# RWKV-7 scan: sums in fixed PSUM tiles, inverses spread, the old state added by TensorE and the new one written by ScalarE

## The chip, the cores and the metric

One Trainium2 chip; the kernel runs on one of its cores. The metric is the device time of one execution in microseconds (us). PE is TensorE's matmul, PEld its weight load, DVE VectorE, ACT ScalarE, POOL GpSimd, SP the engine that issues most DMAs. Each engine executes its instructions in the order in which they stand in its queue.

## The reference

Two layers of an encoder, 1024 tokens of width 1024: attention with an MLP, then RWKV-7 time mixing (16 heads of 64, one scan forward and one backward) with an MLP. What the change touches is the recurrence of the scan:

```python
def rwkv7_scan(r, w, k, v, kk, a):
    def step(state, inp):
        r_t, w_t, k_t, v_t, kk_t, a_t = inp
        sa = jnp.einsum('bhvk,bhk->bhv', state, -kk_t)
        state = (state * w_t[:, :, None, :] + sa[..., None] * (kk_t * a_t)[:, :, None, :]
                 + v_t[..., None] * k_t[:, :, None, :])
        return state, jnp.einsum('bhvk,bhk->bhv', state, r_t)
...
    _, out = lax.scan(step, jnp.zeros((nB, H, N, N), F32), xs)
```

## The kernel before

`trunk` runs attention, an MLP, the projections of the RWKV layer (`rwkv_proj`), the scan (`rwkv_scan`), then the output projection and the second MLP. Only `rwkv_scan` is changed.

The scan works in chunks of 64 tokens (`RC`). A batch (`Batch`) is two pairs of heads (`pr`) in two directions (`d`) over half of the sequence; there are 8 (`NB`). A batch has four groups of 128 tokens (`i`), a group two chunks (`c`). So a group holds 8 steps of `scan`, and four chains (`ci = 2 * pr + d`) run beside each other, each with a state `h` of two 64x64 blocks on the diagonal of a 128x128 tile (`hbd`). Chain 0's second chunk needs the state that its first one left, and so on; the chains don't depend on each other.

One step of a chain, L1384 to L1424, with its sums in three column ranges of one PSUM bank `ch` (a tile `c0` to `c3` for each chain):

1. L1384, ACT: `hd` = the old state times the decay `pc`.
2. L1386 and L1390, PE: the chunk's own sum (`af` and `sv`) plus the old state's part (`zr` and `h`).
3. L1392, ACT, and L1393, DVE: the two 64x64 halves of `y` are copied out, one by each engine.
4. L1395, PE: `af` times `y`; L1397, DVE, and L1398, ACT, copy the halves into `sv`.
5. L1401, PE: the state's update from `bn` and `sv`; L1410, DVE (L1407 where there is no old state): for each half `h_new = sum * pc + hd`.
6. L1416 and L1421, PE: the chunk's output, in the same columns as the update; L1424, ACT, copies it to `ot`.

Around the steps runs work that has no place in the chains. `prep` (DVE, POOL, PE, ACT) makes the operands of a group, 8 groups ahead (`NQ` is 9). `invert` makes the inverse of a batch's 64x64 triangles in two halves: a load `nb` (L1290, two DMAs on SP), 30 pairs of DVE operations (L1295, L1297), stores and loads through DRAM that end in `xt` and in `af`. `post` finishes the inverse on PE (L1350, L1361) before the group's first step. `finish` normalises and stores.

What sets the order: the code is traced step by step. After each step, `side()` lets `b1` (prep), `b2` (post, and what is left of the inverse) and `b3` (finish) go one piece on; at a group's end all three are drained. The whole DVE part of the next batch's inverse is traced at the second group of a batch (L1513 to L1517). A scheduler then orders the traced instructions of each engine by a model of time, with the steps of the scan ahead of the rest (`tc.high_priority(50)`). It also keeps the accesses of different engines to one PSUM bank in the order of the trace.

Of the kernel before, what the change touches and what calls it, by code (L numbers as in the profile page):

```python
# [25 lines left out]
def fsl(i, n):  # L26
    return slice(i * n, (i + 1) * n)
# [1115 lines left out]
def rwkv_scan(tc, g, ap, dr, yd):  # L1143
# [7 lines left out]
    with ExitStack() as es:  # L1151
# [35 lines left out]


        hbd = [[t1.tile([P, P], F32, name=f"h{d}{i}") for i in range(2)] for d in range(4)]
        ybd = [t1.tile([P, 2, RC], F32, name=f"y{d}") for d in range(4)]  # L1190
        for x in sum(hbd, ybd):
            nc.gpsimd.memset(x, 0.0)
        bk = t1.tile([P, 4, 2, 2, RC], F32, name="bk")
        for j in range(2):
            nc.gpsimd.memset(bk[fsl(1 - j, 64), :, j], 0.0)
# [90 lines left out]
        def invert(q):  # L1286

            nb = ip.tile([P, 32, 32], F32, tag="nb", name="nb")
            for i in range(2):
                nc.sync.dma_start(out=nb[fsl(i, 64)], in_=q.nd.rearrange("j u s t -> (j u) s t")[:, fsl(i, 32), fsl(i, 32)])  # L1290
            tmp = ip.tile([P, 512], F32, tag="xtmp", name="xtmp")
            for t in range(30, 0, -1):
                n = 31 - t
                tv = tmp[:, :t * n].rearrange("p (a b) -> p a b", b=n)
                nc.vector.tensor_tensor(out=tv, in0=nb[:, 0:t, t:t + 1].to_broadcast([P, t, n]),  # L1295
                                        in1=nb[:, t:t + 1, t + 1:32].to_broadcast([P, t, n]), op=ALU.mult)
                li = nc.vector.tensor_tensor(out=nb[:, 0:t, t + 1:32], in0=nb[:, 0:t, t + 1:32], in1=tv, op=ALU.add)  # L1297
                if t % 2 == 0:
                    yield
# [67 lines left out]
        def scan(q, i, hs, side):  # L1367
# [3 lines left out]
            for c in range(2):  # L1371
                for pr in range(2):
                    for d in range(2):
                        with tc.high_priority(50):
                            ci = 2 * pr + d
                            u = 2 * pr + c
                            zr, bn, af, pc, sv = w.zr[d][:, u], w.bn[d][:, u], w.af[:, d, u], w.pc[d], w.sv[:, d, u]
                            h = hs[ci]
                            ch = psC.tile([P, 512], F32, tag=f"c{ci}", name=f"c{ci}")
                            last = q.half == 1 and i == 3 and c == 1  # L1380
                            y = ybd[ci]
                            if h is not None and not last:
                                hd = hp.tile([P, P], F32, tag=f"hd{ci}", name=f"hd{ci}", bufs=1)
                                nc.scalar.activation(hd, h, AF.Copy, scale=pc[:, u:u + 1])  # L1384
                            for j in range(2):
                                nc.tensor.matmul(ch[fsl(1 - j, 64), 0:64], lhsT=af[:, j, 0:64], rhs=sv[:, j, :],  # L1386
                                                 start=True, stop=h is None)
                            if h is not None:
                                for j in range(2):
                                    nc.tensor.matmul(ch[fsl(1 - j, 64), 0:64], lhsT=zr[:, 0, :], rhs=h[:, fsl(j, 64)],  # L1390
                                                     start=False, stop=True)
                            nc.scalar.activation(y[0:64, 1], ch[0:64, 0:64], AF.Copy)  # L1392
                            nc.vector.tensor_copy(y[64:128, 0], ch[64:128, 0:64])  # L1393
                            for j in range(2):
                                nc.tensor.matmul(ch[fsl(1 - j, 64), 64:128], lhsT=af[:, j, 0:64], rhs=y[:, j], start=True,  # L1395
                                                 stop=True)
                            nc.vector.tensor_copy(sv[64:128, 0, :], ch[64:128, 64:128])  # L1397
                            nc.scalar.activation(sv[0:64, 1, :], ch[0:64, 64:128], AF.Copy)  # L1398
                            if not last:
                                for j in range(2):  # L1400
                                    nc.tensor.matmul(ch[fsl(j, 64), 128:192], lhsT=bn[:, j, :], rhs=sv[:, j, :], start=True,  # L1401
                                                     stop=True)
                                hn = hbd[ci][c]
                                for j in range(2):
                                    rows = cols = fsl(j, 64)
                                    if h is None:
                                        nc.vector.tensor_scalar(out=hn[rows, cols], in0=ch[rows, 128:192],  # L1407
                                                                scalar1=pc[rows, u:u + 1], scalar2=None, op0=ALU.mult)
                                    else:
                                        nc.vector.scalar_tensor_tensor(out=hn[rows, cols], in0=ch[rows, 128:192],  # L1410
                                                                       scalar=pc[rows, u:u + 1], in1=hd[rows, cols],
                                                                       op0=ALU.mult, op1=ALU.add)
                                hs[ci] = hn

                            for j in range(2):
                                nc.tensor.matmul(ch[fsl(j, 64), 128:192], lhsT=sv[:, j, :], rhs=af[:, j, 64:128],  # L1416
                                                 start=True, stop=h is None)
                            if h is not None:
                                for j in range(2):
                                    rows = fsl(j, 64)  # L1420
                                    nc.tensor.matmul(ch[rows, 128:192], lhsT=h[:, rows], rhs=zr[:, 1, :], start=False,  # L1421
                                                     stop=True)
                            o = w.ot[:, 0, pr, c, :] if d == 0 else w.ot[:, 1, pr, 1 - c, ::-1]
                            nc.scalar.activation(o, ch[:, 128:192], AF.Copy)  # L1424
                        side()
# [79 lines left out]
        for G in range(4 * NB):  # L1505
# [4 lines left out]
            g2 = G + NQ - 1  # L1510
            if G == 0:
                q.gi = gi
            if i == 1 and b + 1 < NB:  # L1513
                bn = bs[b + 1]
                bn.gi = invert(bn)
                while not hasattr(bn, "inv"):
                    next(bn.gi)  # L1517
            if g2 < 4 * NB:
                if g2 % 4 == 0:
                    bs.append(Batch(g2 // 4))  # L1520
# [1 line left out]
            if G + 1 < 4 * NB:  # L1522
                if i == 0:
                    b2.add(post(q, 1), q.gi)
                else:
                    b2.add(post(bs[(G + 1) // 4], (G + 1) % 4))
            if i == 1 and b + 1 < NB:
                b2.add(first(bn))
            n = [0]

            def side():
                n[0] += 1
                b1.step()
                b2.step()
                b3.step()
                if n[0] == 8:
                    b1.drain()
                    b2.drain()
                    b3.drain()
# [159 lines left out]
```

## Time and profile before

| | |
|---|---|
| median of 3 runs | 3665.36 us (3656.43 to 3675.8) |
| profiled execution | 3664.62 us, span from first to last instruction 3662.9 us |
| busy in the span | PE 87%, PEld 71%, DVE 69%, ACT 50%, POOL 48% |
| first and last output copy of the scan (L1424) | 2086.4 and 2859.9 us |
| mean granted PE clock | 0.912 of full speed |

A row of a group reads: line, engine, operation, tile written <- tiles read, shape, count | busy us, mean ns of one | idle us of the engine just ahead of them, with what ended it. Instructions of one engine overlap, so busy time can be less than count times mean. A 64x64 f32 matmul has two records.

### The profile page before, as it was taken

What the parts mean: (1) busy time and instruction counts of PE and PEld (TensorE: products, weight loads), DVE (VectorE), ACT (ScalarE), POOL (GpSimd) and SP (SyncE); (2) the same over time, 40 slices, a digit from 0 to 9 for tenths busy, and PEclk for the clock granted to TensorE, in tenths of its full rate; (3) what the DMA queues carried; (4) which work ended last, traced back from release to release, by engine and by line L of the source; (5) the groups of instructions that cost most, each with busy time, mean ns of one, the idle gap of its engine ahead of it and who ended that gap; (6) DMA issues with size and microseconds to landing.
All of it is one profiled execution on the core that took longest, in us unless ns stands there. A gap on an engine that the chain in (4) does not pass through costs nothing. (4 is left out here: it accounts for less than half of the span.)

```text
span 3662.9 us, 61199 instructions
## 1 busy us (share of the span) xinstructions
PE 3175.4 (87%) x22168; PEld 2587.1 (71%) x22168; DVE 2529.6 (69%) x4649; ACT 1849.7 (50%) x4244; POOL 1768.2 (48%) x1610
## 2 busy tenths in 40 slices
PE   7999998899999888888887687788777889999988
PEld 6788887688777676665566566666665768877766
DVE  3355564744499978977855778887776474449996
ACT  2366564455543347754433365555666445554333
POOL 1000001465598884455566344444431156558887
PEclk9999998899999998999896687778887899999999
DMA  6222214232231133257765354445444423323113
GB/s 202 72 80 81 72 55 171 76 138 108 70 139 37 79 113 107 95 185 232 228 221 155 94 127 107 106 127 122 121 100 133 129 84 135 115 71 131 42 74 115
DMA packets 408204, 425.70 MB, mean 116 GB/s; under 512 B 138155, under 2 KB 321579, under 8 KB 401756
## 3 DMA queue, kind: packets, MB, share of 16 engines
q1 hardware_dynamic: 406716, 417.58, 36.3%
q0 software_dynamic: 1184, 4.20, 0.4%
q8 instruction: 174, 2.85, 0.3%
q14 instruction: 130, 1.06, 0.1%
HBM read 290.83 MB, written 138.20 MB: 117 GB/s over the span
## 5 line engine op out<-in xcount | busy, mean ns | idle before, releaser
L101 PE MATMUL pm<-bhi,lo 128*128 128x512 f32 x840 | 331.8, 398 | 49.5 <-DVE lo L130 49.3
L130 DVE TENSOR_TENSOR lo<-x,hi 128x512 fp32r<-128x512 f32 x300 | 323.3, 1084 | 62.4 <-ACT hi L129 62.0
L129 ACT ACTIVATE hi<-x 128x512 fp32r<-128x512 f32 x300 | 189.1, 631 | 334.1 <-PE pm L100 129.1
L100 PE MATMUL pm<-blo,hi 128*128 128x512 f32 x840 | 330.2, 393 | 7.7 <-POOL blo L130 7.3
L99 PE MATMUL pm<-bhi,hi 128*128 128x512 f32 x840 | 319.2, 393 | 7.1 <-ACT bhi L129 6.7
L127 POOL TENSOR_TENSOR x<-w1r 128x512 f32<-128x512 f32 x160 | 214.6, 1345 | 203.1 <-DVE lo L130 178.3
L130 POOL TENSOR_TENSOR blo<-bx,bhi 128x512 fp32r<-128x512 f32 x138 | 221.1, 1603 | 30.5 <-ACT bhi L129 29.7
L1268 POOL TENSOR_TENSOR af<-af,amask 128x512 f32<-128x512 f32 x128 | 164.8, 1293 | 147.2 <-ACT af L1267 109.3
L101 PEld LDWEIGHTS pm<-bhi,lo 128*128 128x128 f32 x840 | 157.6, 188 | 101.9 <-DVE lo L130 70.8
L1264 PE MATMUL A<-zr,bk 128*128 128x128 f32 x1024 | 189.5, 349 | 44.3 <-DVE bk L1257 38.2
L905 POOL TENSOR_TENSOR wl<-wr,wh 128x512 fp32r<-128x512 f32 (+2 forms) x144 | 162.0, 1136 | 126.3 <-ACT wh L904 94.8
L127 POOL TENSOR_TENSOR bx<-w 128x512 f32<-128x512 f32 x140 | 215.1, 1539 | 9.5
L1264 PEld LDWEIGHTS A<-zr,bk 128*128 128x128 f32 x1024 | 168.1, 252 | 57.2 <-POOL bk L1258 22.0
L127 DVE TENSOR_TENSOR x<-h 128x512 f32<-128x512 f32 x140 | 195.6, 1409 | 5.3 <-ACT h L268 2.7
L100 PEld LDWEIGHTS pm<-blo,hi 128*128 128x128 f32 x840 | 158.4, 189 | 47.7 <-POOL blo L130 14.5
L99 PEld LDWEIGHTS pm<-bhi,hi 128*128 128x128 f32 x840 | 158.4, 189 | 40.0 <-ACT bhi L129 7.6
L99 PE MATMUL mm<-xmh,wh 128*128 128x512 f32 x384 | 163.0, 443 | 10.1 <-ACT wh L904 4.7
L1416 PE MATMUL c<-af,sv 128*64 128x64 f32 x1024 | 96.8, 273 | 74.7 <-DVE h L1410 67.7
L1410 DVE SCALAR_TENSOR_TENSOR h<-c,pc,hd 64x64 f32<-64x64 f32 x448 | 127.0, 284 | 49.6 <-PE c L1401 28.7
L583 ACT ACTIVATE S<-S,mneg 128x256 f32<-128x256 f32 (+2 forms) x256 | 124.7, 499 | 69.1 <-DVE mneg L578 46.2
L335 DVE TENSOR_TENSOR acc<-acc,pm 128x512 f32<-128x512 f32 x256 | 158.1, 675 | 0.3 <-PE pm L101 0.3
L886 DVE SCALAR_TENSOR_TENSOR x<-u,mu,x 128x512 f32<-128x512 f32 x192 | 153.4, 832 | 7.0 <-ACT x L884 4.3
(369 smaller groups left out, 9933.0 us busy)
## 6 DMA issues: line engine op xcount, KB each, us to landing
w1r<-in_mlp_w_dram SPq DMA_DIRECT2D x32, 1024.0 KB, 5.5
w<-in_mlp_w_dram SPq DMA_DIRECT2D x32, 1024.0 KB, 6.7
x<-x SPq DMA_DIRECT2D x64, 386.0 KB, 3.3
hd<-h SPq DMA_DIRECT2D x24, 1024.0 KB, 4.2
h<-hd SPq DMA_DIRECT2D x24, 1024.0 KB, 8.2
wr<-in_w_rkv_dram SPq DMA_DIRECT2D x96, 256.0 KB, 2.8
x<-xo SPq DMA_DIRECT2D x32, 512.0 KB, 3.7
rk<-rk SPq DMA_DIRECT2D x64, 256.0 KB, 3.7
```

The costliest lines, as they stand in the source:

```text
L99: nc.tensor.matmul(out, lhsT=ahi, rhs=bhi, start=start, stop=False)
L100: nc.tensor.matmul(out, lhsT=ahi, rhs=blo, start=False, stop=False)
L101: nc.tensor.matmul(out, lhsT=alo, rhs=bhi, start=False, stop=stop)
L127: add.tensor_tensor(out=y, in0=x, in1=blocks[term[2]], op=ALU.add if term[1] == "+" else ALU.subtract)
L129: nc.scalar.activation(hi, x, AF.Copy)
L130: sub.tensor_tensor(out=lo, in0=x, in1=hi, op=ALU.subtract)
L335: dve.tensor_tensor(out=a, in0=a, in1=banks[j], op=ALU.add if sign == "+" else ALU.subtract)
L886: nc.vector.scalar_tensor_tensor(out=x, in0=at(2 * i), scalar=mu[:, i, c, kt:kt + 1], in1=x, op0=ALU.mult, op1=ALU.add)
L905: nc.gpsimd.tensor_tensor(out=wlo, in0=wr, in1=whi, op=ALU.subtract)
L1264: nc.tensor.matmul(ps[:, fsl(u, P)], lhsT=bk[:, u, j].rearrange("p a b -> p (a b)"), rhs=zr[:, u].rearrange("p a b -> p (a b)"), start=Tru ...
L1268: nc.gpsimd.tensor_tensor(out=o, in0=o, in1=consts["amask"].unsqueeze(1).to_broadcast([P, 4, P]), op=ALU.mult)
L1410: nc.vector.scalar_tensor_tensor(out=hn[rows, cols], in0=ch[rows, 128:192], scalar=pc[rows, u:u + 1], in1=hd[rows, cols], op0=ALU.mult, op ...
```

## The change

The four banks `chs` are taken once and set to 0 by DVE. `y` is one 128x128 tile for the two halves, the first sums go to a block each of a 128x128 range whose other two blocks stay 0, and ACT copies it in one instruction. The old state is added on PE, by a matmul with the identity into the columns of the update (256 to 384), and ACT multiplies the sum by `pc` and writes the new 128x128 state; `hd` and DVE's part in the state are gone. `af y` goes to columns 192 to 256. The output keeps columns 128 to 192, now apart from the update. The DVE part of the next batch's inverse is traced in pieces: its load after the batch's first step, two of the 30 pairs after each of the steps 4 to 18, the rest with the DMAs after step 20.

```diff
--- before.py
+++ after.py
@@ -1187,9 +1187,13 @@
 
 
         hbd = [[t1.tile([P, P], F32, name=f"h{d}{i}") for i in range(2)] for d in range(4)]
-        ybd = [t1.tile([P, 2, RC], F32, name=f"y{d}") for d in range(4)]
-        for x in sum(hbd, ybd):
+        yst = [t1.tile([P, 2, RC], F32, name=f"y{d}") for d in range(4)]
+        for x in sum(hbd, []):
             nc.gpsimd.memset(x, 0.0)
+
+        chs = [psC.tile([P, 512], F32, name=f"c{d}") for d in range(4)]
+        for x in chs:
+            nc.vector.memset(x, 0.0)
         bk = t1.tile([P, 4, 2, 2, RC], F32, name="bk")
         for j in range(2):
             nc.gpsimd.memset(bk[fsl(1 - j, 64), :, j], 0.0)
@@ -1289,6 +1293,7 @@
             for i in range(2):
                 nc.sync.dma_start(out=nb[fsl(i, 64)], in_=q.nd.rearrange("j u s t -> (j u) s t")[:, fsl(i, 32), fsl(i, 32)])
             tmp = ip.tile([P, 512], F32, tag="xtmp", name="xtmp")
+            yield
             for t in range(30, 0, -1):
                 n = 31 - t
                 tv = tmp[:, :t * n].rearrange("p (a b) -> p a b", b=n)
@@ -1376,42 +1381,31 @@
                             u = 2 * pr + c
                             zr, bn, af, pc, sv = w.zr[d][:, u], w.bn[d][:, u], w.af[:, d, u], w.pc[d], w.sv[:, d, u]
                             h = hs[ci]
-                            ch = psC.tile([P, 512], F32, tag=f"c{ci}", name=f"c{ci}")
+                            ch = chs[ci]
                             last = q.half == 1 and i == 3 and c == 1
-                            y = ybd[ci]
-                            if h is not None and not last:
-                                hd = hp.tile([P, P], F32, tag=f"hd{ci}", name=f"hd{ci}", bufs=1)
-                                nc.scalar.activation(hd, h, AF.Copy, scale=pc[:, u:u + 1])
+                            y = yst[ci]
+                            rs = [fsl(1 - j, 64) for j in range(2)]
                             for j in range(2):
-                                nc.tensor.matmul(ch[fsl(1 - j, 64), 0:64], lhsT=af[:, j, 0:64], rhs=sv[:, j, :],
+                                nc.tensor.matmul(ch[rs[j], fsl(j, 64)], lhsT=af[:, j, 0:64], rhs=sv[:, j, :],
                                                  start=True, stop=h is None)
                             if h is not None:
                                 for j in range(2):
-                                    nc.tensor.matmul(ch[fsl(1 - j, 64), 0:64], lhsT=zr[:, 0, :], rhs=h[:, fsl(j, 64)],
+                                    nc.tensor.matmul(ch[rs[j], fsl(j, 64)], lhsT=zr[:, 0, :], rhs=h[:, fsl(j, 64)],
                                                      start=False, stop=True)
-                            nc.scalar.activation(y[0:64, 1], ch[0:64, 0:64], AF.Copy)
-                            nc.vector.tensor_copy(y[64:128, 0], ch[64:128, 0:64])
+                            nc.scalar.activation(y.rearrange("p j t -> p (j t)"), ch[:, 0:P], AF.Copy)
                             for j in range(2):
-                                nc.tensor.matmul(ch[fsl(1 - j, 64), 64:128], lhsT=af[:, j, 0:64], rhs=y[:, j], start=True,
-                                                 stop=True)
-                            nc.vector.tensor_copy(sv[64:128, 0, :], ch[64:128, 64:128])
-                            nc.scalar.activation(sv[0:64, 1, :], ch[0:64, 64:128], AF.Copy)
+                                nc.tensor.matmul(ch[rs[j], 192:256], lhsT=af[:, j, 0:64], rhs=y[:, j], start=True, stop=True)
+                            nc.vector.tensor_copy(sv[64:128, 0, :], ch[64:128, 192:256])
+                            nc.scalar.activation(sv[0:64, 1, :], ch[0:64, 192:256], AF.Copy)
                             if not last:
+                                if h is not None:
+                                    nc.tensor.matmul(ch[:, 256:384], lhsT=g.ident, rhs=h, start=True, stop=False)
                                 for j in range(2):
-                                    nc.tensor.matmul(ch[fsl(j, 64), 128:192], lhsT=bn[:, j, :], rhs=sv[:, j, :], start=True,
-                                                     stop=True)
+                                    nc.tensor.matmul(ch[fsl(j, 64), 256 + 64 * j:320 + 64 * j], lhsT=bn[:, j, :], rhs=sv[:, j, :],
+                                                     start=h is None, stop=True)
                                 hn = hbd[ci][c]
-                                for j in range(2):
-                                    rows = cols = fsl(j, 64)
-                                    if h is None:
-                                        nc.vector.tensor_scalar(out=hn[rows, cols], in0=ch[rows, 128:192],
-                                                                scalar1=pc[rows, u:u + 1], scalar2=None, op0=ALU.mult)
-                                    else:
-                                        nc.vector.scalar_tensor_tensor(out=hn[rows, cols], in0=ch[rows, 128:192],
-                                                                       scalar=pc[rows, u:u + 1], in1=hd[rows, cols],
-                                                                       op0=ALU.mult, op1=ALU.add)
+                                nc.scalar.activation(hn, ch[:, 256:384], AF.Copy, scale=pc[:, u:u + 1])
                                 hs[ci] = hn
-
                             for j in range(2):
                                 nc.tensor.matmul(ch[fsl(j, 64), 128:192], lhsT=sv[:, j, :], rhs=af[:, j, 64:128],
                                                  start=True, stop=h is None)
@@ -1510,11 +1504,9 @@
             g2 = G + NQ - 1
             if G == 0:
                 q.gi = gi
-            if i == 1 and b + 1 < NB:
+            if i == 0 and b + 1 < NB:
                 bn = bs[b + 1]
                 bn.gi = invert(bn)
-                while not hasattr(bn, "inv"):
-                    next(bn.gi)
             if g2 < 4 * NB:
                 if g2 % 4 == 0:
                     bs.append(Batch(g2 // 4))
@@ -1524,8 +1516,6 @@
                     b2.add(post(q, 1), q.gi)
                 else:
                     b2.add(post(bs[(G + 1) // 4], (G + 1) % 4))
-            if i == 1 and b + 1 < NB:
-                b2.add(first(bn))
             n = [0]
 
             def side():
@@ -1533,6 +1523,13 @@
                 b1.step()
                 b2.step()
                 b3.step()
+
+                at = 8 * i + n[0]
+                if b + 1 < NB and (at == 1 or 4 <= at <= 18):
+                    next(bn.gi)
+                if at == 20 and b + 1 < NB:
+                    for _ in first(bn):
+                        pass
                 if n[0] == 8:
                     b1.drain()
                     b2.drain()
```

The built order of PE in the middle of the scan, before. `c_` with a number is the bank of one step; `y_17480` to `y_17483` and `h_17472` to `h_17479` belong to chains 0 to 3.

```order
L1401 MATMUL c_23117<-sv,bn_19857 64x64 x2
L1401 MATMUL c_23237<-sv,bn_20302 64x64 x2
L1386 MATMUL c_23318<-sv,af 64x64 x2
L1390 MATMUL c_23318<-h_17475,zr_20301 64x64 x2
L1416 MATMUL c_23088<-af,sv 64x64 x2
L1421 MATMUL c_23088<-zr_19854,h_17476 64x64 x2
L1416 MATMUL c_23117<-af,sv 64x64 x2
L1421 MATMUL c_23117<-zr_19855,h_17478 64x64 x2
```

PE at about the same place in the changed kernel, where `c_17492` to `c_17495` are the four fixed banks.

```order
L1410 MATMUL c_17494<-af,sv 64x64 x2
L1415 MATMUL c_17494<-zr_20083,h_17477 64x64 x2
L1355 MATMUL B<-xt,af 32x32 x5
L1280 MATMUL A<-ident,bk 128x64 x3
L1410 MATMUL c_17495<-af,sv 64x64 x2
L1415 MATMUL c_17495<-zr_20084,h_17479 64x64 x2
L1402 MATMUL c_17492<-h_17472,ident 128x128
L1404 MATMUL c_17492<-sv,bn_20085 64x64 x2
L1397 MATMUL c_17493<-y_17481,af 64x64 x2
```

The identity matmul (L1402) stands just ahead of the update's (L1404); the output's (L1410, L1415) still come after the update of their own step.

DVE before, where an inverse (L1295, L1297) meets the steps:

```order
L1397 COPY sv<-c_19970 64x64
L1410 SCALAR_TENSOR_TENSOR h_17474<-c_19912,pc_18017,hd_19913 64x64 x2
L1297 TENSOR_TENSOR nb<-nb,xtmp 128x30
L1257 TENSOR_TENSOR bk<-x,ipr 64x4x64
L1295 TENSOR_TENSOR xtmp<-nb 128x58
L1257 TENSOR_TENSOR bk<-x,ipr 64x4x64
L1297 TENSOR_TENSOR nb<-nb,xtmp 128x29x2
L1295 TENSOR_TENSOR xtmp<-nb 128x84
L1297 TENSOR_TENSOR nb<-nb,xtmp 128x28x3
L1295 TENSOR_TENSOR xtmp<-nb 128x108
L1410 SCALAR_TENSOR_TENSOR h_17476<-c_19970,pc_18016,hd_19971 64x64 x2
```

DVE after, at such a place again:

```order
L1398 COPY sv<-c_17492 64x64
L1300 TENSOR_TENSOR xtmp<-nb 128x220
L1398 COPY sv<-c_17493 64x64
L1302 TENSOR_TENSOR nb<-nb,xtmp 128x20x11
L1261 TENSOR_TENSOR bk<-x,ipr 64x4x64
L1300 TENSOR_TENSOR xtmp<-nb 128x228
L1398 COPY sv<-c_17494 64x64
L1261 TENSOR_TENSOR bk<-x,ipr 64x4x64
L1302 TENSOR_TENSOR nb<-nb,xtmp 128x19x12
L1300 TENSOR_TENSOR xtmp<-nb 128x234
L1302 TENSOR_TENSOR nb<-nb,xtmp 128x18x13
```

The steps leave DVE one copy each (L1398); the halves of `y` and of the state are gone from its queue.

ACT before:

```order
L1398 ACTIVATE sv<-c_22694 64x64
L1267 ACTIVATE af<-A 128x4x128
L1424 ACTIVATE ot<-c_22658 128x64
L1392 ACTIVATE y_17482<-c_22723 64x64
L1278 ACTIVATE bn_22463<-A 128x4x64
L1392 ACTIVATE y_17483<-c_22752 64x64
L1278 ACTIVATE bn_22463<-A 128x4x64
L1384 ACTIVATE hd_22873<-h_17475,pc_19859 128x128
L1392 ACTIVATE y_17480<-c_22791 64x64
L1339 ACTIVATE sv<-B 64x8x64 x2
```

ACT after, in the same part of the scan:

```order
L1407 ACTIVATE h_17479<-c_17495,pc_19413 128x128
L1399 ACTIVATE sv<-c_17492 64x64
L1399 ACTIVATE sv<-c_17493 64x64
L1395 ACTIVATE y_17482<-c_17494 128x128
L1271 ACTIVATE af<-A 128x4x128
L1418 ACTIVATE ot<-c_17495 128x64
L1407 ACTIVATE h_17472<-c_17492,pc_19734 128x128
L1435 ACTIVATE osq<-ot 128x512
L1407 ACTIVATE h_17474<-c_17493,pc_19735 128x128
L1399 ACTIVATE sv<-c_17494 64x64
```

L1384 (`hd`) is gone; L1407, the new state, now stands in the queue between the copies of other chains, and L1395 copies all of `y`.

## The prediction

> **What bounds the kernel now.** The change touches only the scan stage, so I first placed that stage in the span, with the view of one source line (the copy of a step's output, L1424, one per chain and step; columns: count, duration ns min/median/max, first and last start) and with the busy time of the engines in that stretch (length, then PE, PEld, DVE, ACT, POOL busy, PE clock, DMA share, GB/s).
>
> ```profile
> L1424 ACT ACTIVATE ot<-c x256: 197/220/235, 2086.4 to 2859.9; 128x64 f32<-128x64 f32 x128
> 2088.00:2862.00 774.00, 614.63 (x9966) 499.19 (x9967) 598.77 (x1708) 463.26 (x1553) 287.49 (x356) 0.80 0.45 116
> ```
>
> The stage is 774 us of the 3662.9. PE is busy 79% of it, DVE 77%, ACT 60%: no engine is full, so waits count. Busy time in shorter stretches shows two regimes. First five that hold the bulk of an inverse, then two with almost none of it; under the sum of the five stands the same sum for L1397 alone, which runs once per step.
>
> ```profile
> 2205.00:2269.50 64.50, 48.47 (x644) 40.02 (x643) 54.14 (x142) 35.39 (x118) 23.29 (x29) 0.72 0.38 104
> 2615.00:2674.00 59.00, 43.74 (x694) 35.54 (x692) 51.69 (x144) 33.89 (x113) 24.54 (x31) 0.83 0.44 111
> sum 293.50, PE 226.94 PEld 186.20 DVE 257.18 ACT 165.88 POOL 119.93; mean PE 45.39 PEld 37.24 DVE 51.44 ACT 33.18 POOL 23.99
> sum 293.50, DVE 17.99; mean DVE 3.60
> 2490.00:2509.00 19.00, 17.02 (x358) 14.41 (x357) 12.81 (x39) 12.99 (x48) 10.71 (x14) 1.00 0.63 153
> 2694.00:2709.00 15.00, 15.00 (x277) 12.76 (x276) 9.14 (x30) 10.28 (x35) 9.34 (x10) 0.97 0.55 122
> ```
>
> In the five (293.5 us) DVE is busy 257.2, 88%, against PE's 77%: DVE sets the pace. In the two short ones PE is busy 90% and 100%, DVE 67% and 61%. The waits of the stage (engine and line that waited, for whom: us, times, longest) say the same:
>
> ```profile
> ACT hd L1384 <- DVE h L1410: 96.9, 115, 4.1
> ACT sv L1398 <- DVE sv L1397: 77.7, 91, 3.7
> PE c L1416 <- DVE h L1410: 67.7, 78, 4.4
> PE c L1395 <- DVE y L1393: 37.3, 41, 5.0
> PE c L1401 <- ACT sv L1398: 25.3, 31, 2.8
> ```
>
> PE's three largest waits, 130.3 us of its 159 idle, end with a chain's DVE copy (the last through ACT, which waits for DVE's half of `sv`). That DVE was busy elsewhere, not slow, shows in the timeline of one such wait (start, duration): chain 0's ACT half of `y` (ACT L1392) is done at 2355.97, its DVE half starts at 2360.20.
>
> ```profile
> 2355.77 0.20 ACT L1392 ACTIVATE y<-c 64x64 f32<-64x64 f32 x1
> ```
> ```profile
> 2357.48 0.94 DVE L1252 TENSOR_TENSOR zr<-x,rk 128x256 f32<-128x256 f32 x1
> 2358.34 0.32 DVE L1295 TENSOR_TENSOR xtmp<-nb 128x168 f32<-128x168 f32 x1
> 2358.59 0.86 DVE L1257 TENSOR_TENSOR bk<-x,ipr 64x256 f32<-64x256 f32 x2
> 2359.48 0.33 DVE L1297 TENSOR_TENSOR nb<-nb,xtmp 128x168 f32<-128x168 f32 x1
> 2359.85 0.32 DVE L1295 TENSOR_TENSOR xtmp<-nb 128x150 f32<-128x150 f32 x1
> 2360.20 0.23 DVE L1393 COPY y<-c 64x64 f32<-64x64 f32 x1
> ```
>
> **The change part by part.** Durations come from groups of the stage (busy us, mean ns | idle before it):
>
> ```profile
> L1410 DVE SCALAR_TENSOR_TENSOR h<-c,pc,hd 64x64 f32<-64x64 f32 x448 | 127.0, 284 | 49.6 <-PE c L1401 28.7 <-ACT y L1392 4.2 <-PE c L1390 2.6
> L1393 DVE COPY y<-c 64x64 f32<-64x64 f32 x252 | 54.1, 226 | 21.5 <-ACT y L1392 18.2
> L1407 DVE TENSOR_SCALAR h<-c,pc 64x64 f32<-64x64 f32 x24 | 6.8, 283 | 1.9 <-PE c L1401 0.9 <-PE c L1416 0.6
> L1384 ACT ACTIVATE hd<-h,pc 128x128 f32<-128x128 f32 x220 | 87.5, 399 | 107.7 <-DVE h L1410 96.9 <-DVE h L1407 8.4
> L1424 ACT ACTIVATE ot<-c 128x64 f32<-128x64 f32 x255 | 53.6, 216 | 16.0 <-PE c L1421 12.7 <-PE c L1416 0.3 <-PE c L1386 0.2
> L1392 ACT ACTIVATE y<-c 64x64 f32<-64x64 f32 x252 | 51.2, 211 | 24.4 <-PE c L1390 22.1
> L1278 ACT ACTIVATE bn<-A 128x256 f32<-128x256 f32 x92 | 33.6, 373 | 5.1 <-PE A L1276 4.8
> L1267 ACT ACTIVATE af<-A 128x512 f32<-128x512 f32 x92 | 52.8, 590 | 28.4 <-PE A L1264 19.5 <-PE c L1416 8.2 <-issue 0.2
> L1445 ACT ACTIVATE osq<-L,gneps 128x512 f32<-128x512 f32 x31 | 21.2, 683 | 20.8 <-PE L L1443 20.6
> L1264 PE MATMUL A<-zr,bk 128*128 128x128 f32 x736 | 125.0, 325 | 4.7 <-DVE zr L1252 1.8 <-DVE bk L1257 1.4 <-DVE xtmp L1295 0.5
> ```
>
> DVE loses 127.0 + 54.1 + 6.8 = 188 us of work, 598.8 to 411 (53% of 774). A step loses 2 x 284 + 226 = 794 ns of DVE and one whole hand-over (`y` went ACT, then DVE).
>
> ACT loses `hd` (87.5) and gains the new state, 128x128 from PSUM with a scale per partition. That form isn't in the trace. 128x64 takes 216 and 128x256 takes 373, so 128x128 lies on the line between them at 268; a per-partition operand adds 683 - 590 = 93 (L1445 against L1267): 361 ns, bounds 268 and 399 (`hd`, the same shape with the same kind of scale). 248 of them are 89.5 us. `y` as one 128x128 copy costs 268 - 211 = 57 more, 252 times, 14 us. ACT goes 463 to 480: no change of load, but it now stands in the chain four times a step.
>
> PE gains 224 identity matmuls 128x128 in f32. The nearest is L1264, also 128x128 f32: its 736 records are two for each matmul, 125.0 / 736 = 0.17 us each, so 0.34 us a matmul and 76 us in all (615 to 691, 89%). In the new order it stands directly ahead of the state's own matmuls and behind the same wait for `sv`, so it can't run early, and lies on the chain.
>
> What does not change: the sums of one chain still share one bank, in the built order the output matmul still waits for the copy of the state (now ACT's), and the next step's first matmul for the output copy. Fixed tiles alone remove no wait; I cost them at 0. The spread inverses keep all 60 DVE operations of a batch. The load of `nb`, two DMAs that hold SP's queue (below), moves up by up to a group, past loads for groups far ahead; its DVE work ends 1 to 7 steps earlier in the order. The wait that could shorten is that of the post-inverse matmuls for `xt`:
>
> ```profile
> 2401.44 5.18 SPq L1290 DMA_DIRECT2D nb<-nd  x2
> L1350 PE MATMUL B<-xt,af 32*32 32x32 f32 x960 | 29.6, 203 | 3.5 <-ACT sv L1339 2.3 <-DMA xt<-xd 1.1
> 1947.73 1.04 DVE L1250 TENSOR_TENSOR zr<-x,rk 128x256 f32<-128x256 f32 x1 [2.87 <-DMA y<-y]
> ```
>
> 1.1 us in all: -1 at best; if the earlier `nb` load held the loads behind it for its whole 5.18 us in each of 7 batches, +36. I take 0, nearest the row, as those loads have whole groups to spare. The four memsets of the banks (DVE, 128x512, once) stand before the third `prep`, where DVE idles 2.87 us (last row): 0, at most 3.
>
> **The sum.** (1) In the five DVE-bound stretches, 17.99 us / 226 ns = 80 steps lose 80 x 794 = 64 us of DVE. PE has 293.5 - 226.9 = 67 us of idle there for 80 x 0.34 = 27 of identity work. I take three quarters, -48 (bounds 0 and -64), since other waits then end last. (2) In the other 480 us the share of the 130.3 us of DVE-made PE waits is 480/774, 81 us; the copy comes from a less loaded queue, or from ACT, and I take half, -40 (bounds 0 and -81). (3) The other 144 identities cost 49 us of PE; PE's remaining idle takes half: +24 (bounds 0 and +49). (4) The longer `y`: 63 steps of a chain x 57 ns, +4. Together -60: 3664.6 (the profiled execution's time; the median of the runs, 3665.4, is the same) - 60 = **3605 us**.
>
> Two rules of the Trainium skill bear on the size. Its page Perfetto Trace Analysis, Identifying the Most-Contended Engine, says that matmul busy time is a bad measure of PE's headroom; by that the 89% would overstate PE, term (3) would be near 0 and the time 3581. The trace agrees as far as the two short stretches go (PE 90% and 100% "busy" at 19 and 15 us for about the same work).
>
> **The rivals.** *PE takes over.* If PE's busy time is real occupancy, terms (1) and (2) are eaten by the 76 us: -48 - 40 + 76 + 4 = -8, 3657, no change. For it: PE is at 90 to 100% in the short stretches. Against it: the same kind of work took 15 us in one and 19 in the other with PE nominally full in both.
>
> *The clock rises too.* PE's clock is 0.72 in a stretch with long waits and 1.00 in one without; at 0.80 on average it stretches every matmul. If the shorter waits lift it to 0.90, PE's 615 us become 546, 68 less, of which half lies on the path: another -34, 3571; all of it, 3537. I take 3550. For it: waits of 4 to 5 us (4.4 and 5.0 in the rows) are just the ones that go. Against it: 2205 to 2269 and 2615 to 2674 have the same DVE share and clocks of 0.72 and 0.83. The Trainium skill, TensorE: Matmul & The Clock Gate, Part 1, has the mechanism: half clock by default and after an idle window of about 3.4 us, full clock after a busy one.
>
> *ACT's queue becomes the bound: slower.* ACT runs in order and stops at its half of `sv` until DVE's half is done: 77.7 us over 91 stops, 0.85 each. Now the new state stands in that queue, behind other chains' `sv`. If each of a chain's 62 states meets one such stop, that is 62 x 0.85 = 53 us, and the identity is 56 x 0.34 = 19; the loop is shorter by 226 + 568 - 361 - 57 = 376 ns, 62 times, -23. Net +49: 3714. It decides once the state waits longer at ACT than it did at DVE by 376 - 340 = about 40 ns beyond what the lighter DVE queue gives back. Against it: DVE, for which ACT stops, loses a third of its work, and the largest stop, `hd`'s 96.9 us, goes.
>
> **How the numbers follow.** Forecast (about 3575 to 3640) 0.50; clock 0.20; PE takes over 0.17; ACT 0.13. Below 0.5% (18 us) a measurement can't tell the two apart. Faster: the first two and a little of the third, 0.74; same 0.14; slower 0.12. The range reaches from the sum with the far ends of (1) and (2), 3664.6 - 64 - 81 = 3520, a little lowered for the clock, 3515, to 3662, which takes in most of "PE takes over" and leaves the slower rival out.
>
> **What would show it.** In the changed kernel's profile: the stage from the first to the last output copy some 60 us shorter; DVE 410 us there; the identity at 0.17 us a record; the state's copy at about 360 ns; no long waits of PE for DVE. The inverse stretches should shrink most and the PE-full ones hardly. I am wrong if the stretches with the inverse keep 55 to 60 us, if ACT's new waits are as long as DVE's were, or if PE's clock moves by more than 0.05.

## The result, and the profile after

The changed kernel takes 3605.73 us (median of 4 runs, 3597.65 to 3608.16), 0.9833 of the time before, with an interval of 0.9802 to 0.9864: about 61 us less. Its profiled execution took 3597.65 us, with a span of 3595.9 us and a PE clock of 0.933 over the span (before 3664.62, 3662.9 and 0.912). A profile is of one execution, here the fastest of the four, and for e3 and e11 below the slowest of four, so small differences between two profiles say little.

First the stage again, in the changed kernel, with the two views that placed it before: the copy of a step's output, and busy time by stretch (length, then PE, PEld, DVE, ACT, POOL, PE clock, DMA share, GB/s). The second and third stretch split the stage: the first seven batches, beside each of which the next batch's inverse runs, and the last batch, which has none beside it.

```profile
L1418 ACT ACTIVATE ot<-c x256: 197/224/269, 2085.2 to 2792.0; 128x64 f32<-128x64 f32 x128
```
```profile
2085.00:2792.00 707.00, 648.65 (x10416) 528.08 (x10414) 420.18 (x960) 466.91 (x1567) 289.66 (x355) 0.90 0.49 127
2085.00:2733.00 648.00, 597.12 (x9446) 487.70 (x9446) 397.25 (x907) 422.60 (x1417) 280.60 (x347) 0.90 0.50 125
2733.00:2792.00 59.00, 51.54 (x974) 40.38 (x972) 22.94 (x53) 44.31 (x151) 9.06 (x9) 0.97 0.47 143
```

The same two stretches of before:

```profile
2086.00:2800.00 714.00, 567.38 (x9076) 463.16 (x9078) 560.85 (x1589) 422.65 (x1414) 281.32 (x348) 0.80 0.46 115
2800.00:2860.00 60.00, 47.23 (x908) 35.79 (x906) 39.73 (x126) 41.35 (x143) 5.59 (x7) 0.83 0.38 120
```

The stage is 67 us shorter, all of the 67 us between the two profiled executions. The seven batches with an inverse beside them give 66 of these (714 to 648 us), the last one 1 (60 to 59). DVE falls from 77% busy to 59%, PE rises from 79% to 92% and ACT from 60% to 66%. The clock rises from 0.80 to 0.90.

Second the groups that the change made or touched (us busy, mean ns | idle before, by whom ended), and under them the stage's waits (engine and line that waited, for whom: us, times, longest):

```profile
L1402 PE MATMUL c<-h,ident 128*128 128x128 f32 x448 | 117.5, 347 | 31.1 <-ACT sv L1399 30.6
L1268 PE MATMUL A<-zr,bk 128*128 128x128 f32 x736 | 116.9, 306 | 3.7 <-DVE zr L1256 2.5 <-DVE bk L1261 0.9
L1407 ACT ACTIVATE h<-c,pc 128x128 f32<-128x128 f32 x236 | 84.7, 364 | 57.9 <-PE c L1404 56.4
L1410 PE MATMUL c<-af,sv 128*64 128x64 f32 x1008 | 82.8, 244 | 4.7 <-ACT sv L1399 2.6 <-ACT h L1407 1.7
L1389 PE MATMUL c<-sv,af 128*64 128x64 f32 x1000 | 82.4, 243 | 7.2 <-ACT ot L1418 7.2
L1395 ACT ACTIVATE y<-c 128x128 f32<-128x128 f32 x252 | 65.3, 270 | 12.4 <-PE c L1393 8.3 <-PE c L1389 1.8 <-PE c L1404 0.5
```
```profile
DVE sv L1398 <- PE c L1397: 94.1, 64, 5.4
ACT sv L1399 <- DVE sv L1398: 89.4, 67, 4.9
ACT h L1407 <- PE c L1404: 56.4, 96, 2.8
PE c L1402 <- ACT sv L1399: 30.6, 22, 3.7
```

The direction of the waits has turned. Before, PE's longest waits ended with a DVE copy (67.7, 37.3 and 25.3 us); now DVE waits 94 us and ACT 56 us for PE, and PE has one wait of size left, the 30.6 us ahead of the identity. Both new ACT copies take what was worked out for them, 364 ns (361) and 270 ns (268). The identity does not: 117.5 us busy over 448 records is 0.26 us each, where the prediction had 0.17 from L1264.

### The profile page after: what moved, and what is told of

It reads as the page before. It is cut to its first block, busy times and chain, and to the rows that moved or that the text cites. A ratio compares the mean times of both kernels' runs of the same rounds, so it can differ in the third digit from the quotient of the medians.

```text
span 3595.9 us, 61432 instructions
## 1 busy us (share of the span) xinstructions
PE 3213.8 (89%) x22616; PEld 2618.0 (73%) x22616; DVE 2357.0 (66%) x3917; ACT 1853.7 (52%) x4260; POOL 1778.8 (49%) x1606
## 5 line engine op out<-in xcount | busy, mean ns | idle before, releaser
L1268 PE MATMUL A<-zr,bk 128*128 128x128 f32 x1024 | 181.1, 336 | 44.5 <-DVE bk L1261 40.1
L1268 PEld LDWEIGHTS A<-zr,bk 128*128 128x128 f32 x1024 | 158.5, 238 | 54.8 <-POOL af L1272 21.5
L1261 DVE TENSOR_TENSOR bk<-x,ipr 64x256 f32<-64x256 f32 x128 | 118.2, 924 | 70.8 <-PE A L1280 62.2
L1398 DVE COPY sv<-c 64x64 f32<-64x64 f32 x256 | 55.2, 226 | 163.9 <-PE c L1397 94.1
```

The lines of the kernel that those rows point to most:

```text
L1268: nc.tensor.matmul(ps[:, fsl(u, P)], lhsT=bk[:, u, j].rearrange("p a b -> p (a b)"), rhs=zr[:, u].rearrange("p a b -> p (a b)"), start=Tru ...
```

## The experiments

Each ran beside the kernel before on the same chip, and each ratio, with its 95% interval, is against that; a gain in us is the ratio's share of 3665. "Stage" is from the first to the last output copy, read as above.

### The identity, taken out and put in

**e1: the changed kernel without the identity.** What is left out of the new state is the old one.

```diff
-if h is not None:
-    nc.tensor.matmul(ch[:, 256:384], lhsT=g.ident, rhs=h, start=True, stop=False)
 for j in range(2):
     nc.tensor.matmul(ch[fsl(j, 64), 256 + 64 * j:320 + 64 * j], lhsT=bn[:, j, :], rhs=sv[:, j, :],
-                     start=h is None, stop=True)
+                     start=True, stop=True)
```

> The changed kernel without the identity matmul: the old state is left out of the new one, all else is computed. In the changed kernel's profile the identity is busy on PE for 117.5 us of a stage of 707, and PE is busy 92% of it. Theory PE is full: it is paid nearly in full, at least 80 us go, about 3505 to 3525. Theory of the prediction (half of it lies in PE's idle time): 40 to 60 us go, 3545 to 3565. Theory clock (PE's clock rose from 0.80 to 0.90 because PE is denser): with less work it falls back to 0.80 to 0.85, and only 15 to 35 us go, 3570 to 3590.

Measured: 3564.83 us, 0.9732 [0.9714, 0.9750]. Its stage:

```profile
2084.00:2751.00 667.00, 553.32 (x9966) 460.05 (x9966) 403.87 (x959) 455.02 (x1567) 290.74 (x356) 0.88 0.53 136
```

In its place the identity costs 0.0101 of the time, 37 us (41 by the two medians), a third of its 117.5 us of busy time. All else together brought 98 us.

**e7: the kernel before, with the identity added** into columns that nothing reads.

```diff
 if not last:
+    if h is not None:
+        nc.tensor.matmul(ch[:, 256:384], lhsT=g.ident, rhs=h, start=True, stop=True)
```

> The kernel before with the same identity matmul added into columns of the bank that nobody reads; nothing else changes, DVE keeps its work. It is on the chain as in the change. Theory PE is full everywhere: 76 to 117 us more, 3740 to 3780. Theory of the prediction (DVE sets the pace, PE has 159 us of idle): 25 to 45 more, 3690 to 3710. Theory clock: the denser PE gets a clock of 0.85 or more in the stage and that pays it back, 3650 to 3675.

Measured: 3696.40 us, 1.0088 [1.0073, 1.0103], 32 us more. The stage, and the identity in it:

```profile
2088.00:2890.00 802.00, 710.56 (x10426) 568.33 (x10426) 588.17 (x1715) 465.85 (x1555) 288.24 (x355) 0.84 0.44 112
```
```profile
L1401 PE MATMUL c<-h,ident 128*128 128x128 f32 x448 | 128.0, 374 | 11.0 <-ACT sv L1398 10.4
```

In the kernel before PE had 159 us of idle in the stage, and yet 128 us of busy time cost 32: idle time of PE on the average does not cover an instruction that stands in each chain. The clock rose by 0.04 and didn't pay for it.

**e2: the changed kernel, the identity in two blocks of 64x64** (the state's other two blocks are 0).

```diff
-    nc.tensor.matmul(ch[:, 256:384], lhsT=g.ident, rhs=h, start=True, stop=False)
+    for j in range(2):
+        nc.tensor.matmul(ch[fsl(j, 64), 256 + 64 * j:320 + 64 * j], lhsT=g.ident[fsl(j, 64), fsl(j, 64)],
+                         rhs=h[fsl(j, 64), fsl(j, 64)], start=True, stop=False)
```

> The changed kernel with the identity matmul only on the two 64x64 blocks that hold the state, one matmul for each, which as other such pairs should run beside each other: about half of PE's time for it, 60 us less. Theory PE is full: 45 to 60 us go, 3545 to 3560. Theory of the prediction: 20 to 30, 3575 to 3585. Theory clock: under 15, 3590 to 3605.

Measured: 3606.86 us, 0.9846 [0.9829, 0.9862], no gain. The stage, and the identity in it:

```profile
2092.00:2802.00 710.00, 635.71 (x10862) 520.05 (x10858) 426.59 (x960) 465.86 (x1567) 287.78 (x355) 0.87 0.49 126
```
```profile
L1403 PE MATMUL c<-h,ident 64*64 64x64 f32 x896 | 80.3, 256 | 16.2 <-ACT sv L1399 16.1
```

The identity's busy time falls by 37 us, but PE's by 13 only, and the clock from 0.90 to 0.87: the rest of PE's work took 24 us more. (Over the whole span the changed kernel's four runs have clocks of 0.927 to 0.933 and those of e2 0.924 to 0.926, so the clock is lower in e2, but by less.) If PE's busy time set the end, a third of 37 us or more would have come back. Why it did not stays open; the lower clock goes with it, but the run cannot say which of the two is the cause.

### One part of the change at a time

**e8: the kernel before, with the four fixed banks alone.**

```diff
+chs = [psC.tile([P, 512], F32, name=f"c{d}") for d in range(4)]
+for x in chs:
+    nc.vector.memset(x, 0.0)
...
-ch = psC.tile([P, 512], F32, tag=f"c{ci}", name=f"c{ci}")
+ch = chs[ci]
```

> The kernel before with nothing but the four fixed banks (and their memsets). Prediction: the order of the accesses to a bank is the same, so no change, 3655 to 3675. Rival: the release of a whole tile held the next step's first matmuls, 3630 or less.

Measured: 3666.59 us, 1.0001 [0.9991, 1.0011]. The fixed tiles are worth nothing by themselves, as costed.

**e4: the kernel before, with the spread inverse alone; e3: the changed kernel with the old inverse.** e4's edit is this, and e3's is the same undone.

```diff
 tmp = ip.tile([P, 512], F32, tag="xtmp", name="xtmp")
+yield
...
-if i == 1 and b + 1 < NB:
+if i == 0 and b + 1 < NB:
     bn = bs[b + 1]
     bn.gi = invert(bn)
-    while not hasattr(bn, "inv"):
-        next(bn.gi)
...
-if i == 1 and b + 1 < NB:
-    b2.add(first(bn))
...
+at = 8 * i + n[0]
+if b + 1 < NB and (at == 1 or 4 <= at <= 18):
+    next(bn.gi)
+if at == 20 and b + 1 < NB:
+    for _ in first(bn):
+        pass
```

> The kernel before with the inverse traced in pieces as in the change and nothing else. Prediction: no change, 3655 to 3675. Rival, the spread is a good part of the gain: 3645 or less. Rival, the earlier load of nb holds SP's queue: 3680 or more.

> The changed kernel with the inverse traced as before, in one piece at a batch's second group. Prediction: no change against the changed kernel, 3595 to 3615. Rival, the spread is a good part of the gain: 3625 or more.

Measured: e4 3653.04 us, 0.9962 [0.9947, 0.9976], 14 us less than before; e3 3615.21 us, 0.9861 [0.9840, 0.9881], 10 us more than after, though these two intervals overlap. The spread's own gain is shown by e4, and e3 is in line with it. e4's stage has nearly the same busy times as before's, and the same clock of 0.80:

```profile
2088.00:2849.00 761.00, 605.24 (x10015) 496.54 (x10016) 597.93 (x1701) 461.53 (x1558) 286.39 (x356) 0.80 0.46 118
```

So no work went and no clock rose, only waits became shorter. Which ones isn't settled: ACT's two largest waits for DVE are 21 us shorter together, PE's three that end with DVE only 5.

**e5: the changed kernel with the old state** (`hd` on ACT, two DVE instructions for the new state, no identity; the update is back in the output's columns 128 to 192; the spread and the one copy of `y` stay).

```diff
+if h is not None and not last:
+    hd = hp.tile([P, P], F32, tag=f"hd{ci}", name=f"hd{ci}", bufs=1)
+    nc.scalar.activation(hd, h, AF.Copy, scale=pc[:, u:u + 1])
...
-if h is not None:
-    nc.tensor.matmul(ch[:, 256:384], lhsT=g.ident, rhs=h, start=True, stop=False)
...
-nc.scalar.activation(hn, ch[:, 256:384], AF.Copy, scale=pc[:, u:u + 1])
+for j in range(2):
...
+        nc.vector.scalar_tensor_tensor(out=hn[rows, cols], in0=ch[rows, 128:192],
+                                       scalar=pc[rows, u:u + 1], in1=hd[rows, cols],
+                                       op0=ALU.mult, op1=ALU.add)
```

> The changed kernel with the state as before: hd on ACT, the sum of sum*pc and hd on DVE, no identity; y stays one ACT copy, inverses stay spread. Taking the identity away from the changed kernel gave 41 us, so all that the change gave without it is about 100. Theory DVE load: the gain goes with the DVE work removed, 54 of 188 us, so 0.29 x 100 = 29 us below the kernel before, 3630 to 3645. Rival, hand-overs: the y copy was one of the chain's two DVE hand-overs that go, so half, 3605 to 3620. Rival, the state's part is worth nothing and y is all: 3565 to 3580.

Measured: 3629.22 us, 0.9902 [0.9880, 0.9924], 36 us less than before. The stage:

```profile
2090.00:2821.00 731.00, 594.27 (x9996) 490.48 (x9992) 544.01 (x1440) 469.08 (x1556) 285.10 (x355) 0.82 0.48 122
```

DVE is at 74% of the stage, and the clock back at 0.82.

**e6: the changed kernel with `y` in two halves again**, ACT's and then DVE's.

```diff
-nc.scalar.activation(y.rearrange("p j t -> p (j t)"), ch[:, 0:P], AF.Copy)
+nc.scalar.activation(y[0:64, 1], ch[0:64, 64:128], AF.Copy)
+nc.vector.tensor_copy(y[64:128, 0], ch[64:128, 0:64])
```

> The changed kernel with y copied in two halves as before, ACT then DVE; new state with identity, spread inverses. Theory DVE load: 134 of 188 us of work gone gives 72, less 41 for the identity: about 30 below the kernel before, 3625 to 3640. Rival, hand-overs: 50 - 41, 3650 to 3660. Rival, y is all: the identity's price alone is left, 3690 to 3705.

Measured: 3652.13 us, 0.9962 [0.9949, 0.9974], 14 us less than before and 47 more than after. Its stage and two of its waits:

```profile
2089.00:2851.00 762.00, 687.41 (x10426) 554.23 (x10423) 468.33 (x1220) 461.51 (x1568) 284.41 (x356) 0.85 0.46 118
```
```profile
DVE y L1396 <- ACT y L1395: 85.7, 78, 4.3
ACT sv L1400 <- DVE sv L1399: 83.7, 87, 4.4
```

DVE is down at 468 us of 762, and still little is won: its copy of `y` waits 85.7 us for ACT's half, where before it waited 18.2. Here a lighter DVE brought nothing to chains that must go through ACT and then DVE for one value. One copy of `y` is worth 47 us here; with the old state it is worth 22 (e5's 36 less the spread's 14). The parts don't add up: the state's move without the copy of `y` gives nothing beside the spread's 14 (e4 and e6 have the same ratio), the copy of `y` without the state's move 22, and both 47. By the intervals each of these is good to some 10 us. Neither theory covers both runs: e5 came out as "DVE load" had it, e6 as "hand-overs".

### Where the next wait is

**e9, e10, e11: `sv` copied by one engine.** In all three the sums of `af y` go to a 128x128 range and `sv` is written whole, which puts zeros in the two blocks of `sv` that hold `v`; what is left out is `v`'s part of the update and of the output. e9 copies on ACT, e10 on DVE, e11 is e10 with e2's two blocks.

```diff
-    nc.tensor.matmul(ch[rs[j], 192:256], lhsT=af[:, j, 0:64], rhs=y[:, j], start=True, stop=True)
-nc.vector.tensor_copy(sv[64:128, 0, :], ch[64:128, 192:256])
-nc.scalar.activation(sv[0:64, 1, :], ch[0:64, 192:256], AF.Copy)
+    nc.tensor.matmul(ch[rs[j], 384 + 64 * j:448 + 64 * j], lhsT=af[:, j, 0:64], rhs=y[:, j], start=True, stop=True)
+nc.scalar.activation(sv, ch[:, 384:512].rearrange("p (j t) -> p j t", j=2), AF.Copy)
```

> The changed kernel with the same step taken once more: the second sums go to 64x64 blocks of a 128x128 range (columns 384 to 512) and ACT alone copies all of sv in one instruction; DVE has no part in the chains. Theory hand-overs (a chain's step pays for each engine it waits for in turn): the two waits of 94 us (DVE for PE) and 89 us (ACT for DVE) become one, 40 to 70 us less, 3535 to 3565. Theory DVE load: DVE is only 59% busy, its last 54 us are worth little, 3590 to 3610. Rival, ACT full: 14 us more work and everything in its queue, 3615 or more.

> As the run beside it, but DVE alone copies all of sv (about 290 ns), ACT loses 51 us of work. The number of hand-overs is the same as there. Theory hand-overs: 3535 to 3565 as well. Theory load (what counts is which engine has work waiting): better than with ACT, since ACT is 66% busy and DVE 59%, by 10 to 30 us. Rival, the inverse's DVE operations hold the copy up: 3590 to 3610.

> As the run with sv on DVE, with the identity on the two 64x64 blocks. On the changed kernel that halving of PE's work was worth nothing. Theory PE is the next bound once a hand-over is gone: 15 to 40 us below the run with sv on DVE. Theory chain (the identity costs by its length in the chain, which two blocks don't shorten): the same within 10 us.

Measured: e9 3598.29 us, 0.9828 [0.9814, 0.9843]; e10 3585.96 us, 0.9797 [0.9778, 0.9816]; e11 3603.02 us, 0.9843 [0.9809, 0.9877]. The stages of e10 and e11:

```profile
2083.00:2781.00 698.00, 640.94 (x10417) 519.23 (x10416) 407.93 (x960) 443.15 (x1317) 290.16 (x356) 0.93 0.50 129
```
```profile
2089.00:2814.00 725.00, 664.37 (x10865) 538.22 (x10864) 408.58 (x961) 446.60 (x1318) 289.96 (x356) 0.86 0.48 125
```

"Hand-overs" expected 3535 to 3565 us of e9 and e10. The hand-over of `sv` from DVE to ACT is not what holds the changed kernel: without it, 0.0005 (ACT) or 0.0036 (DVE) of the time go, the one well inside after's interval, the other with an interval that overlaps it. PE is busy 92% of the stages of e10 and e11. The two blocks again bring nothing, and again with a lower clock (over the whole span 0.922 to 0.935 in e11's four runs, 0.936 to 0.941 in e10's).

**e12: the changed kernel without the identity, the new state by one DVE instruction.** The sum stays 128x128, `hd` is ACT's again, and DVE multiplies the sum by `pc` and adds `hd` in one instruction instead of two.

```diff
+hd = hp.tile([P, P], F32, tag=f"hd{ci}", name=f"hd{ci}", bufs=1)
+nc.scalar.activation(hd, h, AF.Copy, scale=pc[:, u:u + 1])
...
-    nc.tensor.matmul(ch[:, 256:384], lhsT=g.ident, rhs=h, start=True, stop=False)
...
-nc.scalar.activation(hn, ch[:, 256:384], AF.Copy, scale=pc[:, u:u + 1])
+nc.vector.scalar_tensor_tensor(out=hn, in0=ch[:, 256:384], scalar=pc[:, u:u + 1],
+                               in1=hd, op0=ALU.mult, op1=ALU.add)
```

> The changed kernel without the identity, the new state made by one DVE operation on 128x128 (sum*pc + hd, about 350 ns) where the kernel before took two on 64x64 (568), hd on ACT as before; y one ACT copy, inverses spread. PE loses 117 us of busy time, DVE gains 87. Theory PE is now the bound and DVE has room: the identity's 41 us come back and DVE's 87 us (507 of 700) cost less than that, 3575 to 3595. Theory DVE load (100 us of gain for 188 us of DVE work): 29 + 0.53 x 49 = 55 below the kernel before, 3605 to 3615. Rival, the state on DVE waits behind the inverse as before: 3620 or more.

Measured: 3590.05 us, 0.9797 [0.9780, 0.9815], 74 us less than before. The stage and the new instruction:

```profile
2087.00:2792.00 705.00, 589.82 (x9976) 485.58 (x9972) 481.19 (x1201) 465.19 (x1554) 288.40 (x355) 0.83 0.50 127
```
```profile
L1412 DVE SCALAR_TENSOR_TENSOR h<-c,pc,hd 128x128 f32<-128x128 f32 x223 | 75.1, 348 | 51.0 <-PE c L1405 35.2 <-ACT ot L1424 6.0 <-PE c L1400 2.0
```

One DVE instruction of 348 ns does the work of two of 284 ns, and no work goes to PE, which is at 84%. By the ratios this is 13 us faster than the changed kernel; the intervals overlap at their ends, so that it beats the kernel before is shown, and that it beats the changed one is likely but not settled.

## Why the prediction was right

It gave 3605 us and the median is 3605.73. The total fits better than its parts, and so well by luck:

| Step of the prediction | Predicted | By the runs |
|---|---|---|
| DVE's relief, terms (1) and (2), with the longer `y` (4) | -48 - 40 + 4 = -84 | -84: e1's -98 less the spread's -14 |
| The identity (3) | +24 | +37 (e1 against after), +32 (e7) |
| Spread inverses | 0 | -14 (e4), -10 (e3) |
| Fixed tiles | 0 | 0 (e8) |
| Sum | -60 | -61 |

The right-hand sum is no check of its own: its first two rows are both reckoned from e1, and with e4's 14 they give back the measured 61.

**DVE sets the pace before: right in the main.** The gain lies where the inverse also loads DVE (66 us of 67), PE's waits for DVE went, and e5 shows 22 us that come without any move of the state. In the traces, the state's instruction starts 1.37 us on average after the last matmul of its sum in the kernel before (DVE), and 0.44 us in the changed one (ACT), over 240 steps each. What shows little is the other half of term (2), a DVE that answers sooner: its copy of `sv` starts 1.06 us after the last matmul of its sum before and 0.94 after (means of 256 steps, medians 0.67 and 0.22). The -84 takes the spread's gain to be the same with and without the other edits; e4's 14 and e3's 10 agree with that, though e3's is not clear of noise. How it divides into (1) and (2) can't be read, as the spread lays the inverse over the whole batch. For the same reason no stretch is left that holds the bulk of an inverse, and the sign "if the stretches with the inverse keep 55 to 60 us" can't be read; a batch went from 102 us to 93 (714 / 7 and 648 / 7).

**The identity: right in kind, mis-sized.** It was to cost a third of its busy time, 24 of 76 us, and it costs a third, 37 of 117.5. What failed is the 0.17 us a record, taken from L1264. That group's records come eight in a row (736 for the 92 copies of L1267) and overlap each other: in the changed kernel 736 records of 306 ns are 225 us, in 116.9 us of busy time (L1268). The identity's two records stand alone among 64x64 matmuls. They last hardly longer, 347 ns, but overlap less: 448 of them are 155 us, in 117.5 us of busy time. Why they overlap less wasn't tried. The prediction's upper bound, +49 for the part that no idle time covers, holds both measured costs.

**The spread: missed.** "0, -1 at best" looked for a single wait that it could shorten, that for `xt`; but the 60 DVE instructions of an inverse, traced in one piece, also stand ahead of the steps' copies, and apart they may hold them up less. No run shows that this is how e4's 14 us come. The two misses, +13 and -14, cancel.

**The clock: the condition that was to prove the forecast wrong came true,** since it moved by 0.10, and yet the time is the forecast's and not that rival's 3550. The rival's mechanism did take place: PE's work without the identity fell from 614.6 to 648.7 - 117.5 = 531.2 us. But the gain does not hang on it alone. From e5 to e12 the clock goes from 0.82 to 0.83 and the time falls by 0.0105, 38 us, with DVE's 544 us down to 481; in e4 the clock stays at 0.80 and 14 us go; in e7 it rises by 0.04 and 32 us come. How many of the 84 us are due to the clock stays open, since no run holds it fixed; the prediction's sum has no term for it, so terms (1) and (2) may be too large by that much.

**PE takes over: in part.** PE is now the busiest engine and the others wait for it, as that rival said. But it priced the identity at its whole busy time, and the runs at a quarter (e7) to a third (e1). e2 and e11 add that less of this busy time is no gain. What the prediction held against this rival was misread: its two short stretches are not the same work, as the one of 19 us has 358 PE records and the one of 15 us has 277, so both take 53 to 54 ns a record. The Trainium skill, Perfetto Trace Analysis, Identifying the Most-Contended Engine, says that matmul busy time is not a good measure of how close a kernel is to the roofline, its bound at full use of an engine; e2 fits that (37 us less busy for the identity, 0 gained). That the 89% would overstate PE and the identity cost near 0 was the prediction's own inference, and 37 and 32 us were measured.

**ACT's queue: did not come.** ACT's stops at `sv` take a little longer than before (89.4 us against 77.7), and a stop is dearer than the rival had it (89.4 / 67 = 1.33 us against 0.85). But PE waits only 1.7 us for the state's copy ahead of the output matmul and 7.2 us for the output copy (the rows of L1410 and L1389), and its largest wait for ACT is 30.6 us in all, where the one for DVE was 67.7. The state's copy starts 0.44 us on average after its sum, and in half of the steps within 0.05 us. That the state would meet a stop in each step was the error.

## What to carry to other kernels

Price a matmul that stands alone in a dependent chain by one that stands alone too, not by one out of a row, and count a quarter to a third of it as lost even where its engine is idle a fifth of the time, as it was here. Moving work off the engine that sets the pace paid here only when the chain's other hand-over went with it: the state's move gave nothing with `y` in halves (e6 against e4) and 25 us with `y` whole (e5 against after). Before work is given to a third engine, try whether the busy one can do it in one wide instruction instead of two narrow ones; here that was, by its median, the fastest version that leaves nothing of the computation out.

## What the runs showed of the hardware

**A busy PE at a low clock.** The same part of a batch in the changed kernel and in e3 (old inverse), by stretch:

```profile
2472.00:2526.00 54.00, 48.60 (x714) 39.36 (x712) 41.52 (x100) 34.42 (x111) 24.09 (x30) 0.87 0.54 140
```
```profile
2476.00:2545.00 69.00, 61.68 (x733) 48.89 (x733) 41.43 (x102) 36.83 (x118) 26.22 (x32) 0.71 0.48 118
```

Nearly as many records, PE 90% and 89% busy, and yet a clock of 0.87 and 0.71, and 54 and 69 us. Inside e3's stretch there are 20.48 us in which PE reads as busy throughout and has half the clock:

```profile
2483.85:2504.33 20.48, 20.48 (x229) 16.86 (x227) 14.19 (x35) 10.91 (x37) 6.35 (x8) 0.50 0.33 81
```

A high busy share does not by itself bring the full clock back, and the share is itself raised by the low clock: a record takes 61.68 / 733 = 84 ns of busy time in e3's stretch and 48.60 / 714 = 68 ns in the other. The Trainium skill, TensorE: Matmul & The Clock Gate, Part 1, has it back after a busy window of about 3.4 us; either PE's busy share in the profile isn't what that gate counts, or more is needed, and no run here tells.

**DVE held up while POOL runs.** In the kernel before, one DVE instruction of a line whose mean is 0.45 us in the changed kernel took 3.63 us (start, duration, in the timeline):

```profile
2353.92 3.63 DVE L1250 TENSOR_TENSOR zr<-x,rk 128x256 f32<-128x256 f32 x1
2354.10 1.26 POOL L1268 TENSOR_TENSOR af<-af,amask 128x512 f32<-128x512 f32 x1
2355.32 0.72 POOL L1258 TENSOR_TENSOR bk<-x,ipr 64x256 f32<-64x256 f32 x1
2356.01 1.27 POOL L1268 TENSOR_TENSOR af<-af,amask 128x512 f32<-128x512 f32 x1
```

It ends at 2357.55, 0.27 us after the third of three POOL instructions in a row. The Trainium skill, SBUF — State Buffer, SBUF: two separate sides, says that a DVE instruction with two inputs in SBUF and a POOL one that reads SBUF share a port as an exclusive lock, which goes to the one that starts first. The rows agree in part: the DVE instruction lasts as long as the three, but it starts 0.18 us ahead of the first, and so POOL should have been the one to wait. No run tried it. The mean of this line's 46 went from 718 to 449 ns with the change, but that of another such DVE line (`bk`, L1257 before and L1261 after) went from 733 to 849. In sum DVE's relief does not come from here: the work left to it was 411 us by subtraction and is 420.

```profile
L1250 DVE TENSOR_TENSOR zr<-x,rk 128x256 f32<-128x256 f32 x46 | 33.0, 718 | 10.7 <-PE c L1421 4.3 <-ACT y L1392 3.6 <-PE c L1395 1.1
```
```profile
L1254 DVE TENSOR_TENSOR zr<-x,rk 128x256 f32<-128x256 f32 x46 | 20.7, 449 | 38.5 <-PE c L1415 29.6 <-ACT x L1251 4.1 <-PE c L1404 2.5
```
```profile
L1257 DVE TENSOR_TENSOR bk<-x,ipr 64x256 f32<-64x256 f32 x90 | 66.0, 733 | 6.4 <-PE A L1276 3.0 <-ACT y L1392 1.6
```
```profile
L1261 DVE TENSOR_TENSOR bk<-x,ipr 64x256 f32<-64x256 f32 x90 | 76.4, 849 | 26.3 <-PE A L1280 21.9 <-ACT y L1395 2.0 <-ACT h L1407 0.5
```
